# Spreading a position bias over query rows: single-partition transfers on ScalarE's queue, or scratch in HBM on GpSimd's

## The chip, the cores and the metric

One core of a Trainium2 chip runs the whole program: two layers of a first transformer block and two of a second, on 256 tokens of 1024 features. The metric is device time in microseconds (us), from the launch to the end of the program.

## What is computed

All of it is float32. In the part that the change touches, a feed-forward product is followed by an attention in windows, whose scores get a learned bias by relative position (cut from the reference):

```python
for i in range(DEPTH):                                    # DEPTH = 2
    h = x + 0.5 * swiglu(rms_norm(x, norm_ffn1[i]), w_ffn1_in[i], w_ffn1_out[i])
    u = rms_norm(h, norm_mix[i])
    q, k, v, c, g = jnp.split(u @ w_in[i], splits, axis=-1)
    ...
    y_attn = window_attention(q, k, v, sink[i], rel_bias) @ w_attn_out[i]
    ...

def window_attention(q, k, v, sink, rel_bias):            # BLOCK = WINDOW = 128, 8 heads
    ...
    rel = kj[None, :] - BLOCK - qi[:, None]               # qi: 128 query rows, kj: 384 key columns
    bias = rel_bias[t5_buckets(rel)]
    bias = bias.transpose(2, 0, 1).reshape(KV_HEADS, GROUP, BLOCK, 3 * BLOCK)
    s = s + bias[None, None]
    s = jnp.where(valid[None, :, None, None], s, NEG_INF)
    ...
```

The bias depends on `rel` alone. A head therefore needs one line of 511 numbers, of which query row r wants the 384 that begin at 127 - r. The same table serves both layers.

## The kernel before

**Tiling.** Tokens are columns, features are partitions: `h` is 128 x 8 x 256. Every product runs on 128 x 128 weight tiles against 256 columns. For precision each float32 weight is split into a high and a low part, and each tile takes three matmuls (`mm3`, lines 281 to 283).

**The weight stream.** `Stream` loads the weights in the order of a plan, in chunks of 128 x 2048 (1 MB) into three `raw` buffers, by transfers that SyncE's queue issues (line 198). Each chunk has two halves of 1024 columns. For each half ScalarE makes `wh` (line 221) and VectorE makes `wl` (line 222), in three buffers each. A half serves 24 matmuls in an output product. `wh` of a half waits until its `raw` has landed and until the matmuls of the half three before it are done.

**The stage in question.** `swiglu` runs an input product (line 405 writes its hidden values `hh`) and then an output product, `stage_o`, whose four results are added to `h` (line 442) on VectorE and squared for the next norm. The norm's mean goes to GpSimd, which raises it to the power -0.5 (`rt`, line 383). Then `mix1` runs its projections and the window attention, where VectorE reads the bias (line 511). The same stage stands in both layers, and the scheduler places the work of `bias_table()` at its start in layer 0.

**The bias table.** `bias_table()` is called once, after the first feed-forward part of layer 0. Two matmuls (line 1101) turn the one-hot matrix `oh` and the table `rl` into `tps`, 8 heads x 512 positions, and VectorE copies it to `tsb` (line 1103), one head to a partition. Then eight transfers of 192 KB each, issued by ScalarE's queue (line 1107), fill the two `bias` tiles of 128 x 4 x 384: each reads one partition of `tsb` 128 times, one element earlier for each query row, in runs of 384 numbers (1536 bytes).

**What sets the order.** Each engine runs its instructions in the order in which the scheduler wrote them, and an instruction that waits holds all that stand behind it on that engine. A transfer's issue is an instruction of the issuing engine's queue like any other.

Of the kernel before, what the change touches and what calls it, by code (L numbers as in the profile page):

```python
# [10 lines left out]
F32 = mybir.dt.float32  # L11
# [140 lines left out]
def build(ctx: ExitStack, tc: tile.TileContext, ws, xT, pT, vec, rbias, const, out):  # L152
    nc = tc.nc
# [7 lines left out]
    tmp = ctx.enter_context(tc.tile_pool(name="tmp", bufs=1))  # L161
    sm = ctx.enter_context(tc.tile_pool(name="sm", bufs=2))
    psm = ctx.enter_context(tc.tile_pool(name="psm", bufs=4, space=PSUM))
    side = {}

    def stile(shape, name):
        return side["s"].tile(shape, F32, tag="s", name=name)
# [4 lines left out]
    def f32(ap):  # L172
        return ap.bitcast(F32)

# [1 line left out]
    class Stream:  # L176
        RAW, LEAD = 3, 1

# [65 lines left out]

    W = Stream()

# [1 line left out]
    ident = cst.tile([128, 128], F32, name="ident")  # L248
    ones = cst.tile([128, 128], F32, name="ones")
    nv = VEC["_n"]  # L250
# [13 lines left out]
    def vc(name, l, i=0, n=1):  # L264
        a, _ = VEC[name, l]
        return vt[:, a + i:a + i + n]
# [1 line left out]
    mhalf = cst.tile([128, 32], F32, name="mhalf")  # L268
    S.activation(out=mhalf, in_=ones[:, 0:32], func=AF.Copy, scale=-0.5)

# [1 line left out]
    def cut(wh, wl, s):  # L272
        return wh[:, s], None if wl is None else wl[:, s]

# [47 lines left out]
                    mm3(o, (X.hi[k][:, s], X.lo[k][:, s]), (wh[:, a:b], wl[:, a:b]),  # L322
                        k == 0 and first, k == K - 1)

# [1 line left out]
    def new_h():  # L326
        return hp.tile([128, KD, T], F32, tag="h", name="h")

# [84 lines left out]
    def with_phase(name):  # L413
        def wrap(f):
            def go(*a):
                with phase(name) as P:
                    return f(P, *a)
            return go
        return wrap

# [1 line left out]
    @with_phase("ffn")  # L422
    def swiglu(P, l, which, h, norm, rb, nxt):
        hi, lo, A = hidden(P, 22)
# [46 lines left out]
        stage_o("w_down_2", l, 32, 26, A, evac_out)  # L471
        return h2

# [1 line left out]
    cur = {}  # L475

    def atile(name):
# [81 lines left out]
                    V.scalar_tensor_tensor(out=dl[:, j, :], in0=tp[:, j, :], scalar=gc, in1=f32(dh[:, j, :]),  # L559
                                           op0=ALU.mult, op1=ALU.subtract)  # L560

# [1 line left out]
    @with_phase("mix")  # L563
    def mix1(P, l, h, norm, nxt, ple):
        rt, rb = norm.finish()
# [139 lines left out]

        conv()

        # layer norm over channels, then silu
        def chan_sum(src, name):
            s2 = etile(name)  # L710
            V.tensor_tensor(out=s2, in0=src[:, 0:2, :], in1=src[:, 2:4, :], op=ALU.add)
            s1 = etile(name + "b")
            mark[name] = V.tensor_tensor(out=s1[:, 0:1, :], in0=s2[:, 0:1, :], in1=s2[:, 1:2, :], op=ALU.add)
            return s1

        R = tail.enter_context(phase("tail"))
        with tc.high_priority(offset=LN):
# [12 lines left out]
            for ct in range(4):  # L730
                S.activation(out=co[:, ct, :], in_=y[:, ct, :], func=AF.Silu, scale=vc("conv_ln_g", l, ct),
                             bias=vc("conv_ln_b", l, ct))
# [54 lines left out]
        stage_g("w_pe_gate", l, KD, G_PE, norm.act, evac)  # L787
        return h2

# [1 line left out]
    def rope_apply(dst, src, nh, dh, t, off):  # L791
        half = dh // 2
        cos = rope[:, t, off:off + half].unsqueeze(1).to_broadcast([128, nh, half])
        sin = rope[:, t, off + half:off + dh].unsqueeze(1).to_broadcast([128, nh, half])
        x1, x2 = src[:, :, 0:half], src[:, :, half:dh]
        ta = tmp.tile([128, nh, half], F32, tag="ra", name="ra", bufs=2)
        tb = tmp.tile([128, nh, half], F32, tag="rb2", name="rb2", bufs=2)
        tc_ = tmp.tile([128, nh, half], F32, tag="ra", name="ra", bufs=2)
        td = tmp.tile([128, nh, half], F32, tag="rb2", name="rb2", bufs=2)
        V.tensor_tensor(out=ta, in0=x1, in1=cos, op=ALU.mult)  # L800
        V.tensor_tensor(out=tb, in0=x2, in1=sin, op=ALU.mult)
        V.tensor_tensor(out=tc_, in0=x2, in1=cos, op=ALU.mult)
        V.tensor_tensor(out=td, in0=x1, in1=sin, op=ALU.mult)
        V.tensor_tensor(out=dst[:, :, 0:half], in0=ta, in1=tb, op=ALU.subtract)
        V.tensor_tensor(out=dst[:, :, half:dh], in0=tc_, in1=td, op=ALU.add)

    @with_phase("mixers")
    def mix2(P, l, h, norm, nxt):
# [67 lines left out]

            return [job(i) for i in range(3)]

        # mixer B, projections
        cq = P.tile([128, 2, 544], F32, name="cq")  # L880
        proj(G_B[0], [cq[:, t, 0:288] for t in range(2)])
        proj(G_B[1], [cq[:, t, 288:544] for t in range(2)])
# [11 lines left out]
        to_feature(cq[:, :, 0:512], 4, cT[:, 0], cT[:, 1], 0,  # L894
                   gain=lambda j: vc("mla_q_norm_g_2", l, j) if j < 3 else vc("mla_kv_norm_g_2", l))

        # mixer C, projections
        cc = P.tile([128, 2, 768], F32, name="cc")
        for i in range(3):
            proj(G_C[i], [cc[:, t, 256 * i:256 * i + 256] for t in range(2)])  # L900
# [4 lines left out]
        to_T(lambda t, j: cc[:, t, 128 * j:128 * j + 128], cqT[:, 0:2, :], 0, 2, 32 ** -0.5)  # L905
        to_T(lambda t, j: cc[:, t, 128 * j:128 * j + 128], cqT[:, 2:4, :], 2, 2, None)

        # mixer C, attention
        def combine(opc):
            oc = etile("oc")  # L910
            S.activation(out=oc.rearrange("p a b -> p (a b)"), in_=opc.rearrange("p t h d -> p (t h d)"), func=AF.Copy)
            sqc = etile("sqc")
            S.activation(out=sqc, in_=oc, func=AF.Square)
            ssc = sm.tile([128, 8], F32, tag="ssc", name="ssc")
            V.tensor_reduce(out=ssc, in_=sqc.rearrange("p a (h d) -> p (a h) d", d=64), op=ALU.add,
                            axis=mybir.AxisListType.X)
            msc = sm.tile([128, 8], F32, tag="msc", name="msc")
            V.tensor_scalar(out=msc, in0=ssc, scalar1=1.0 / 64, scalar2=1e-5, op0=ALU.mult, op1=ALU.add)
            rsc = sm.tile([128, 8], F32, tag="rsc", name="rsc")
            G.tensor_tensor(out=rsc, in0=msc, in1=mhalf[:, 0:8], op=ALU.pow)  # L920
            V.tensor_tensor(out=o_tok[:, :, 768:1024].rearrange("p a (h d) -> p a h d", d=64),
                            in0=oc.rearrange("p a (h d) -> p a h d", d=64),
                            in1=rsc.rearrange("p (a h) -> p a h", a=2).unsqueeze(3).to_broadcast([128, 2, 4, 64]),
                            op=ALU.mult)
            return lambda: to_feature(o_tok[:, :, 768:1024], 2, ho, lo, 6, gain=lambda j: subg[l])
# [64 lines left out]

        advance(STEPS[0])

        # mixer B, up-projections
        qb = P.tile([128, 2, 576], F32, name="qb")
        Xq = Act([cT[:, 0, k, :] for k in range(3)], [cT[:, 1, k, :] for k in range(3)])
        Xk = Act([cT[:, 0, 3, :]], [cT[:, 1, 3, :]])
# [22 lines left out]

        advance(STEPS[1])  # L1020

        # mixer A
        qa = P.tile([128, 2, 2, 384], F32, name="qa")
        va = P.tile([128, 2, 384], F32, name="va")
        for i in range(2):
# [26 lines left out]
        stage_o("w_o_2", l, KD, 5, Act([ho[:, k, :] for k in range(8)], [lo[:, k, :] for k in range(8)]), evac_o, CBA)  # L1052
        return h2

# [1 line left out]
    nA = Norm("norm_ffn1", 0)  # L1056
    for j in range(4):
        nA.prep(h, j)
# [32 lines left out]
    bias1 = [P1.tile([128, 4, 384], F32, name=f"bias{i}") for i in range(2)]  # L1091
    ple_out = P1.tile([128, 8, T], F32, name="ple")

    # relative position bias of every head, window columns -128..255 around each query block
    def bias_table():
        rl = cst.tile([33, 8], F32, name="rl")
        oh = tmp.tile([33, 512], F32, tag="e", name="oh", bufs=4)
        nc.sync.dma_start(out=rl, in_=rbias)
        nc.sync.dma_start(out=oh, in_=const["onehot"])
        tps = stile([8, 512], "tps")  # L1100
        PE.matmul(tps, rl, oh, start=True, stop=True)
        tsb = tmp.tile([8, 512], F32, tag="e", name="tsb", bufs=4)
        V.tensor_copy(out=tsb, in_=tps)
        for hd in range(8):
            base = tsb[hd:hd + 1, 127:511]
            src = bass.AP(tensor=base.tensor, offset=base.offset, ap=[list(base.ap[0]), [-1, 128], [1, 384]])
            nc.scalar.dma_start(out=bias1[hd // 4][:, hd % 4, :], in_=src)  # L1107

# [1 line left out]
    for l in range(DEPTH):  # L1110
        ple = {}
        _, rb = nA.finish()
# [38 lines left out]
        (nc.scalar if j % 2 else nc.sync).dma_start(out=out[:, 2 * j:2 * j + 2, :], in_=o)  # L1151


# [1 line left out]
def _consts():  # L1155
    ident = np.eye(128, dtype=np.float32)
    i = np.arange(T)
    dist = i[:, None] - i[None, :]
    causal = np.where(dist >= 0, 0.0, NEG2).astype(np.float32)
    mult = ((dist <= 128).astype(int) + (dist % 4 == 0) + (dist % 16 == 0)) * (dist >= 0)  # L1160
    logm = np.where(mult > 0, np.log(np.maximum(mult, 1)), NEG2).astype(np.float32)

    def rows(a):
        return a.reshape(2, 128, -1).transpose(1, 0, 2).reshape(128, -1)

    tabs = []
    for dim in (64, 32):
        half = dim // 2
        inv = (1.0 / (10000.0 ** (np.arange(half, dtype=np.float64) / half)))
        inv = inv.astype(np.float32)  # L1170
        ang = i.astype(np.float32)[:, None] * inv[None, :]
        tabs += [np.cos(ang.astype(np.float64)), np.sin(ang.astype(np.float64))]
    tabs = np.concatenate(tabs + [np.zeros((T, 96))], axis=1).astype(np.float32)
    blob = np.concatenate([ident, rows(causal), rows(logm), rows(tabs)], axis=1)

    rel = np.arange(512) - 255
    n = np.abs(rel)
    nf = np.maximum(n, 1).astype(np.float32)
    big = 8 + (np.log(nf / np.float32(8)) / np.float32(math.log(16)) * np.float32(8)).astype(np.int32)
    big = np.minimum(big, 15)  # L1180
    bucket = np.where(rel > 0, 16, 0) + np.where(n < 8, n, big)
    onehot = np.zeros((33, 512), np.float32)
    inside = n <= 128
    onehot[bucket[inside], np.arange(512)[inside]] = 1.0
    onehot[32, ~inside] = NEG1
    return np.ascontiguousarray(blob, dtype=np.float32), onehot
# [56 lines left out]
```

## Time and profile before

| what | value |
|---|---|
| median of three runs (1792.05 to 1794.16) | 1793.62 us |
| profiled execution, span from first to last instruction | 1792.7 us |
| TensorE busy | 1739.1 us, 97% |
| VectorE busy | 1182.9 us, 66% |
| ScalarE busy | 957.5 us, 53% |
| GpSimd busy | 27.9 us, 2% |
| mean granted TensorE clock | 0.989 of full speed |
| moved by the DMA engines | 302.91 MB, mean 169 GB/s |

The profiled execution is one more execution of the same program; of its own time the profile gives the span, which lies 0.9 us under the median. Busy time counts an engine's work, not the time in which its queue is held by an issue: ScalarE's held queue is named apart (ACTq). In rows of a timeline the columns are start, duration, engine, line, operation, tiles, and in brackets the idle time before with what ended it.

### The profile page before, as it was taken

What the parts mean: (1) busy time and instruction counts of PE and PEld (TensorE: products, weight loads), DVE (VectorE), ACT (ScalarE), POOL (GpSimd) and SP (SyncE); (2) the same over time, 40 slices, a digit from 0 to 9 for tenths busy, and PEclk for the clock granted to TensorE, in tenths of its full rate; (3) what the DMA queues carried; (4) which work ended last, traced back from release to release, by engine and by line L of the source; (5) the groups of instructions that cost most, each with busy time, mean ns of one, the idle gap of its engine ahead of it and who ended that gap; (6) DMA issues with size and microseconds to landing.
All of it is one profiled execution on the core that took longest, in us unless ns stands there. A gap on an engine that the chain in (4) does not pass through costs nothing.

```text
span 1792.7 us, 33450 instructions
## 1 busy us (share of the span) xinstructions
PE 1739.1 (97%) x14132; PEld 1705.3 (95%) x14132; DVE 1182.9 (66%) x1825; ACT 957.5 (53%) x1517; POOL 27.9 (2%) x25
## 2 busy tenths in 40 slices
PE   8996699999999999999999999999999999999998
PEld 8995699999999999999989999999899999999998
DVE  6662279867664866658877665678576557766644
ACT  5441258755444644456855444568555446755543
POOL 0000000000000000000000000000000000000000
PEclk9998799999999999999999999999999999999999
DMA  7557745254555544555334555544255554435552
GB/s 272 177 182 115 133 160 193 78 192 183 188 177 199 184 176 183 188 190 187 118 141 174 182 187 188 187 166 162 72 188 188 189 184 158 150 106 179 187 190 104
DMA packets 45598, 302.91 MB, mean 169 GB/s; under 512 B 5223, under 2 KB 6503, under 8 KB 12936
## 3 DMA queue, kind: packets, MB, share of 16 engines
q1 hardware_dynamic: 44008, 298.68, 47.1%
q10 hardware_dynamic: 1440, 2.10, 2.5%
q8 instruction: 110, 1.80, 0.4%
q14 instruction: 40, 0.33, 0.0%
HBM read 298.14 MB, written 1.05 MB: 167 GB/s over the span
## 4 chain that ended last, share of the span: by engine, by line
PE 91%; ACT 2%; ACTq 2%; DVE 2%; DMA 1%; issue 0%; POOLq 0%; DVEq 0%; SPq 0%
PE m L283 25%; PE m L282 25%; PE m L281 25%; ACTq L1107 2%; PE sp L508 2%; PE pa L283 2%; PE pa L282 2%; PE pa L281 2%; PE op L537 2%; PE m L279 1%; DVE wl L222 1%; PE tp L524 1%; ACT wh L221 1%; DMA raw<-in_ws_dram 1%; PE tpq L834 0%; PE qps L282 0%
## 5 line engine op out<-in xcount | busy, mean ns | idle before, releaser
L222 DVE TENSOR_TENSOR wl<-raw,wh 128x1024 fp32r<-128x1024 f32 (+3 forms) x565 | 674.9, 1198 | 507.4 <-ACT wh L221 505.9
L221 ACT ACTIVATE wh<-raw 128x1024 fp32r<-128x1024 f32 (+3 forms) x565 | 584.4, 1038 | 722.5 <-PE m L282 576.4
L281 PE MATMUL m<-xh,wh 128*128 128x256 f32 x2432 | 684.2, 284 | 7.4 <-ACT wh L221 7.4
L282 PE MATMUL m<-xl,wh 128*128 128x256 f32 x2432 | 687.6, 284 | 0.5 <-DVE xl L348 0.5
L283 PE MATMUL m<-xh,wl 128*128 128x256 f32 x2432 | 681.7, 284 | 0.0
L281 PEld LDWEIGHTS m<-xh,wh 128*128 128x128 f32 x2432 | 465.6, 192 | 8.0 <-ACT wh L221 7.4
L282 PEld LDWEIGHTS m<-xl,wh 128*128 128x128 f32 x2432 | 467.1, 192 | 1.5 <-DVE xl L348 0.9
L283 PEld LDWEIGHTS m<-xh,wl 128*128 128x128 f32 x2432 | 464.0, 192 | 1.3 <-issue 1.3
L281 PE MATMUL m<-hh,wh 128*128 128x256 f32 x1216 | 336.8, 279 | 31.3 <-ACT wh L221 31.3
L282 PE MATMUL m<-hl,wh 128*128 128x256 f32 x1216 | 336.3, 278 | 0.0
L283 PE MATMUL m<-hh,wl 128*128 128x256 f32 x1216 | 332.2, 279 | 1.9 <-DVE wl L222 1.7
L281 PEld LDWEIGHTS m<-hh,wh 128*128 128x128 f32 x1216 | 231.2, 190 | 32.8 <-ACT wh L221 32.8
L282 PEld LDWEIGHTS m<-hl,wh 128*128 128x128 f32 x1216 | 230.9, 190 | 0.0
L283 PEld LDWEIGHTS m<-hh,wl 128*128 128x128 f32 x1216 | 227.5, 190 | 3.3 <-DVE wl L222 3.3
L282 PE MATMUL pa<-wl,xh 128*128 128x256 f32 (+2 forms) x256 | 77.7, 307 | 0.5 <-DVE wl L222 0.5
L281 PE MATMUL pa<-wh,xh 128*128 128x256 f32 (+2 forms) x256 | 77.7, 310 | 0.0
L283 PE MATMUL pa<-wh,xl 128*128 128x256 f32 (+2 forms) x256 | 76.9, 308 | 0.0
L595 ACT ACTIVATE tap<-cpad,vt 128x256 f32<-128x256 f32 x120 | 53.6, 500 | 9.3 <-DVE acc L597 9.3
L606 DVE SCALAR_TENSOR_TENSOR acc<-cpad,vt,acc 128x256 f32<-128x256 f32 x120 | 52.7, 479 | 0.8
L282 PEld LDWEIGHTS pa<-wl,xh 128*128 128x128 f32 x256 | 48.3, 190 | 1.5 <-DVE wl L222 1.1
L281 PEld LDWEIGHTS pa<-wh,xh 128*128 128x128 f32 x256 | 48.1, 190 | 0.9 <-issue 0.7
L283 PEld LDWEIGHTS pa<-wh,xl 128*128 128x128 f32 x256 | 47.8, 190 | 0.4 <-issue 0.3
(255 smaller groups left out, 1882.9 us busy)
## 6 DMA issues: line engine op xcount, KB each, us to landing
raw<-in_ws_dram SPq DMA_DIRECT2D x254, 1024.0 KB, 4.8
raw<-in_ws_dram SPq DMA_DIRECT2D x18, 768.0 KB, 4.3
raw<-in_ws_dram SPq DMA_DIRECT2D x8, 896.0 KB, 4.6
raw<-in_ws_dram SPq DMA_DIRECT2D x2, 944.0 KB, 5.3
raw<-in_ws_dram SPq DMA_DIRECT2D x2, 864.0 KB, 4.6
raw<-in_ws_dram SPq DMA_DIRECT2D x2, 848.0 KB, 4.5
raw<-in_ws_dram SPq DMA_DIRECT2D x3, 512.0 KB, 7.2
bias<-tsb ACTq DMA_DIRECT2D x8, 192.0 KB, 24.4
```

The costliest lines, as they stand in the source:

```text
L221: S.activation(out=h[:, :b - a], in_=t[:, a:b], func=AF.Copy)
L222: V.tensor_tensor(out=lo[:, :b - a], in0=t[:, a:b], in1=f32(h[:, :b - a]), op=ALU.subtract)
L279: PE.matmul(o, wh, xh, start=first, stop=last, skip_group_check=True)
L281: PE.matmul(o, wh, xh, start=first, stop=False, skip_group_check=True)
L282: PE.matmul(o, wh, xl, start=False, stop=False, skip_group_check=True)
L283: PE.matmul(o, wl, xh, start=False, stop=last, skip_group_check=True)
L508: PE.matmul(sp[:, t, :n], q[:, 128 * t:128 * t + 128], k[:, :n], start=True, stop=True, skip_group_check=True)
L524: PE.transpose(tp[:, kt, 128 * t:128 * t + 128], pr[:, t, 128 * kt:128 * kt + 128], ident)
L537: PE.matmul(o[t], pt[:, kt, 128 * t:128 * t + 128], v[kt], start=(kt == 0), stop=(kt == nk - 1), skip_group_check=True)
L595: S.activation(out=pt[:, ct % 2, :], in_=cpad[:, ct, tap:tap + T], func=AF.Copy, scale=vc("conv_w", l, ct * TAPS + tap))
L606: V.scalar_tensor_tensor(out=y[:, ct, :], in0=src, scalar=wc, in1=y[:, ct, :], op0=ALU.mult, op1=ALU.add)
L1107: nc.scalar.dma_start(out=bias1[hd // 4][:, hd % 4, :], in_=src)
```

## The change

The eight transfers leave ScalarE's queue. In their place GpSimd issues ten: `tsb` goes to a line of 8 x 512 in HBM, that line is copied to `rep`, 8 x 128 x 512 in HBM (every head's line 128 times, 2 MB), and from `rep` eight loads fill the bias tiles. Each reads 128 rows of 384 numbers, at a step of 511 numbers, so that each row begins one position earlier in its own copy of the line.

```diff
+    drm = ctx.enter_context(tc.tile_pool(name="drm", bufs=1, space=bass.MemoryType.DRAM))
...
         tsb = tmp.tile([8, 512], F32, tag="e", name="tsb", bufs=4)
         V.tensor_copy(out=tsb, in_=tps)
+        line = drm.tile([8, 512], F32, name="line")
+        nc.gpsimd.dma_start(out=line, in_=tsb)
+        rep = drm.tile([8, 128, 512], F32, name="rep")
+        base = line[0:8, :]
+        src = bass.AP(tensor=base.tensor, offset=base.offset, ap=[[512, 8], [0, 128], [1, 512]])
+        nc.gpsimd.dma_start(out=rep, in_=src)
         for hd in range(8):
-            base = tsb[hd:hd + 1, 127:511]
-            src = bass.AP(tensor=base.tensor, offset=base.offset, ap=[list(base.ap[0]), [-1, 128], [1, 384]])
-            nc.scalar.dma_start(out=bias1[hd // 4][:, hd % 4, :], in_=src)
+            base = rep[hd]
+            src = bass.AP(tensor=base.tensor, offset=base.offset + 127, ap=[[511, 128], [1, 384]])
+            nc.gpsimd.dma_start(out=bias1[hd // 4][:, hd % 4, :], in_=src)
```

The rest of the diff takes out comments; below the added pool the lines of the program move down by one.

ScalarE's instructions in the program before, at the end of layer 0's first input product and the start of the output product (`wh` is the high half of the weights, `raw` the loaded weights):

```order
L405 ACTIVATE hh<-u 128x512
L221 ACTIVATE wh<-raw 128x1024 x3
L1107 DMA bias_150<-tsb 128x1x384
L221 ACTIVATE wh<-raw 128x1024
L1107 DMA bias_150<-tsb 128x1x384 x3
L1107 DMA bias_151<-tsb 128x1x384
L221 ACTIVATE wh<-raw 128x1024
L1107 DMA bias_151<-tsb 128x1x384 x3
L221 ACTIVATE wh<-raw 128x1024 x13
```

The same engine and place in the changed program:

```order
L431 ACTIVATE g<-g 128x512
L406 ACTIVATE hh<-u 128x512
L222 ACTIVATE wh<-raw 128x1024 x18
L347 ACTIVATE xh<-h,vt 128x256 x2
L356 ACTIVATE sq<-h 128x512
```

The 3 + 1 + 1 + 13 splits that stood around the eight issues now stand in one row of 18. On GpSimd, the changed program has from the first norm on:

```order
L384 TENSOR_TENSOR rt<-ms,mhalf 128x2
L1106 DMA line<-tsb 8x512
L1110 DMA rep<-line 1024x1x512
L1114 DMA bias_152<-rep 128x384 x4
L1114 DMA bias_153<-rep 128x384 x4
L384 TENSOR_TENSOR rt<-ms,mhalf 128x2
L637 TENSOR_TENSOR qrs<-qms,mhalf 128x20
```

The ten issues stand between the powers of the first and the second norm of layer 0, where GpSimd had nothing before. TensorE, VectorE and SyncE have the same instructions in the same order as before.

## Rows read from the trace of the kernel before

**Rows 1.** The page's 40 slices of the span: granted TensorE clock in tenths.

```profile
PEclk9998799999999999999999999999999999999999
```

**Rows 2.** The page's chain that ended last, shares by engine and line.

```profile
PE m L283 25%; PE m L282 25%; PE m L281 25%; ACTq L1107 2%; PE sp L508 2%; PE pa L283 2%; PE pa L282 2%; PE pa L281 2%; PE op L537 2%; PE m L279 1%; DVE wl L222 1%; PE tp L524 1%; ACT wh L221 1%; DMA raw<-in_ws_dram 1%; PE tpq L834 0%; PE qps L282 0%
```

**Rows 3.** ScalarE's timeline, layer 0's stage, and the last hh of layer 1.

```profile
140.50 0.63 ACT L405 ACTIVATE hh<-u 128x512 fp32r<-128x512 f32 x1 [2.10 <-DVE u L433]
...
147.77 0.60 ACTq L1107 DMA_DIRECT2D bias<-tsb  x1
...
148.97 20.14 ACTq L1107 DMA_DIRECT2D bias<-tsb  x4
169.23 1.06 ACT L221 ACTIVATE wh<-raw 128x1024 fp32r<-128x1024 f32 x1 [19.22 <-issue]
169.26 21.30 ACTq L1107 DMA_DIRECT2D bias<-tsb  x3
190.66 2.95 ACT L221 ACTIVATE wh<-raw 128x1024 fp32r<-128x1024 f32 x3 [20.37 <-DMA bias<-tsb]
...
746.27 0.63 ACT L405 ACTIVATE hh<-u 128x512 fp32r<-128x512 f32 x1 [2.10 <-DVE u L433]
```

**Rows 4.** Waits from 140 to 235 us: total, times, longest.

```profile
PE m L281 <- ACT wh L221: 31.3, 3, 15.6
...
ACT wh L221 <- DMA raw<-in_ws_dram: 9.2, 2, 8.6
...
PE m L283 <- DVE wl L222: 1.7, 3, 0.8
```

**Rows 5.** VectorE's timeline: tsb, and the stage's first h in each layer.

```profile
147.07 0.67 DVE L1103 COPY tsb<-tps 8x512 f32<-8x512 f32 x1
...
226.92 0.69 DVE L442 SCALAR_TENSOR_TENSOR h<-m,h 128x512 f32<-128x512 f32 x1
...
791.46 0.68 DVE L442 SCALAR_TENSOR_TENSOR h<-m,h 128x512 f32<-128x512 f32 x1
```

**Rows 6.** Windows: length, busy PE, PEld, DVE, ACT, POOL (instructions), PEclk, DMA share, GB/s.

```profile
140.50:226.92 86.42, 53.40 (x399) 51.04 (x398) 21.57 (x19) 18.09 (x18) 0.00 (x0) 0.80 0.76 121
746.27:791.46 45.19, 45.11 (x398) 44.91 (x397) 21.26 (x19) 18.47 (x18) 0.00 (x0) 1.00 0.55 195
```

**Rows 7.** The chain in order of time: start, duration, what.

```profile
145.08 0.95 PE tps L1101 x2
```

**Rows 8.** GpSimd's timeline: rt of the second norm in layers 0 and 1.

```profile
248.27 0.70 POOL L383 TENSOR_TENSOR rt<-ms,mhalf 128x2 f32<-128x2 f32 x1 [227.66 <-DVE ms L381]
...
812.33 0.69 POOL L383 TENSOR_TENSOR rt<-ms,mhalf 128x2 f32<-128x2 f32 x1 [180.39 <-DVE ms L381]
```

**Rows 9.** Instructions on the bias tiles: ns min/median/max, first and last start.

```profile
L511 DVE CUSTOM_DVE_ANT_0 pr<-sp,bias,nsink x32: 471/480/485, 307.1 to 892.5; 128x256 f32<-128x256 f32 x32
L1107 ACTq DMA_DIRECT2D bias<-tsb x8: 530/6226/8425, 147.8 to 183.2; - x8
```

**Rows 10.** DMA from 146 to 206 us: queue's packets, MB, share; KB each, us to landing.

```profile
q10 hardware_dynamic: 1143, 1.57, 71.1%
...
raw<-in_ws_dram SPq DMA_DIRECT2D x5, 1024.0 KB, 14.3
```

**Rows 11.** DMA from 0 to 60 us: KB each, us to landing.

```profile
rope<-in_blob_dram SPq DMA_DIRECT2D x1, 192.0 KB, 8.6
```

**Rows 12.** The page's DMA issues: KB each, median us to landing.

```profile
raw<-in_ws_dram SPq DMA_DIRECT2D x254, 1024.0 KB, 4.8
```

**Rows 13.** ScalarE's and VectorE's timelines in layer 1's stage.

```profile
764.74 1.06 ACT L221 ACTIVATE wh<-raw 128x1024 fp32r<-128x1024 f32 x1 [1.66 <-PE m L282]
...
765.84 1.22 DVE L222 TENSOR_TENSOR wl<-raw,wh 128x1024 fp32r<-128x1024 f32 x1 [1.49 <-ACT wh L221]
```

**Rows 14.** TensorE's timeline after the first stall, first and last matmul of a half.

```profile
170.34 0.58 PE L281 MATMUL m<-hh,wh 128*128 128x256 f32 x1 [13.21 <-ACT wh L221]
...
175.94 0.28 PE L283 MATMUL m<-hh,wl 128*128 128x256 f32 x1
```

## Prediction

> **What bounds the kernel now.** Read the page's 40 slices first: the granted TensorE clock is full everywhere except in two neighbouring slices, at about 134 to 224 us, where it falls to 7 and 8 tenths [rows 1]. Then the chain that ended last: it is TensorE's matmuls nearly everywhere, and the only entry near the top that is neither a matmul nor weight handling is ScalarE's own queue at line 1107, with 2% of the span [rows 2]. Line 1107 issues the eight bias transfers. So the place to look at is one stage, the first feed-forward output product of layer 0.
>
> ScalarE's timeline there shows what happens [rows 3]. The first bias transfer is issued in 0.60 us at 147.77. The next four hold ScalarE's queue for 20.14 us, and the three after them for 21.30 us, until 190.66. Between them stand weight splits (wh, line 221), which run one at 169.23 and the next at 190.66; without wh neither the rest (wl, VectorE) nor the matmuls can go on. TensorE waits 31.3 us in three waits for wh and 1.7 us for wl [rows 4].
>
> How much of that is the transfers' doing can be read from layer 1, which runs the same stage on the same shapes with no bias table. I take as marks the last hidden split of the input product (hh, line 405) and the first residual addition (h, line 442): 140.50 to 226.92 in layer 0, 746.27 to 791.46 in layer 1 [rows 3, 5]. These are 86.42 and 45.19 us; TensorE is busy 53.40 of the one and 45.11 of the other, at mean clocks of 0.80 and 1.00 [rows 6]. So layer 0 is **41.23 us** longer: 33.0 us in which TensorE stands idle, and 8.3 us in which its matmuls take longer, after each stall at the lower clock.
>
> **The change part by part.** *Taken away:* eight DMA issues on ScalarE and the wait for wh behind them. Of the 41.23 us, 0.95 us belong to the two table matmuls at line 1101, which the chain counts at that price [rows 7]; they stay. What goes is 41.23 - 0.95 = **40.3 us**, if the stage then runs as in layer 1. In the built order the instructions of TensorE and VectorE are the same ones in the same order, ScalarE's are the same less the eight issues, and SyncE's loads are the same; so layer 1 is a fair model of what is left.
>
> *Added on GpSimd:* ten issues (line, rep, eight bias), of which rep waits for line to land and the first bias for rep. Ahead of them GpSimd has nothing to do (its idle time before rt is 227.66 us), and next after them stands rt (line 383), at 248.27 before [rows 8] and so about 208 after. No row shows an issue by GpSimd. The nearest are ScalarE's first at 0.60 us and its worst at 8.43 us, a blocked one [rows 3, 9]: ten make 6 to 84 us. I take 1 us each, 10 us, near the first, because what held ScalarE's queue was a backlog of slow transfers that the new source does not have.
>
> *Added on the DMA engines:* rep writes 2 MB from HBM to HBM, bias loads 8 x 192 KB from HBM. The old transfers had 1536-byte runs from one partition: 1143 packets took 71.1% of 16 engines for 60 us [rows 10], that is 0.711 x 16 x 60 / 1143 = 0.60 us each. A load of the same size and run length from HBM, rope, 192 KB, landed in 8.6 us in the crowd of the program's first loads [rows 11]; a weight load of 1 MB lands in 4.8 us [rows 12]. Cheap end for rep: two weight loads, 9.6 us. Dear end: 1024 packets of 0.60 us on 16 engines, 38 us, and doubled if it shares them with the weights, 76 us. The bias loads: 8 of 8.6 us one after another, 69 us, at the dear end, and 1.5 x 4.8 = 7 us at the cheap end. I take 20 us for rep and 20 us for the eight, because source and target are contiguous HBM rows as in the weight loads. Then: tsb ready at 147.8 [rows 5], line landed at about 151 (an estimate: one issue and a landing like that of a small load), rep at 171, last bias issue at 180, last landing near 195. The cover is 13 us or more before rt at 208, and, as the bias is first read by line 511 at 307.1 before [rows 9], so at 266.8 after, about 70 us before that.
>
> [...]
>
> *The weights beside it.* The weight queue has to keep 1 MB per 5.44 us. In layer 1 a wh starts every 2.72 us (1.06 us of work after 1.66 us of waiting for TensorE); its wl is done 2.3 us after the start (764.74 to 765.84 + 1.22) [rows 13] and frees the raw buffer; the same buffer's next wh comes five halves later, 13.6 us. That leaves 11.3 us for a landing that takes 4.8, so 6.5 us of slack, and TensorE takes a half two halves after its buffer came free, 5.4 - 2.3 = 3.1 us more. A weight load may therefore double to 9.6 us and cost nothing; if the cover is gone, it costs rival A. I take nothing for it.
>
> *Sum.* The profiled execution's span is 1792.7; 1792.7 - 40.3 = 1752.4. The median of the runs shown is 0.9 us above that span, so the forecast for the median is **1753.3 us**. The layers stay alike behind the stage: from the first h to the next rt it is 21.35 us in layer 0 and 20.87 in layer 1 [rows 5, 8], so what this comparison leaves open is about 0.5 us, and I leave it out of the sum.
>
> **The rivals.** *A: the weights come late beside rep and bias.* For it: in the bias stretch of before, weight loads landed in a median of 14.3 us, against 4.8 [rows 10, 12], and ScalarE waited 9.2 us for raw [rows 4]. Against it: those shared the engines with 0.60 us packets from one partition. At 14.3 us, three buffers turn over in 14.3 + 5.0 = 19.3 us in place of 16.3, 1 us lost per chunk of 5.44 us; over 76 us that is 14 chunks, 14 us: up to **1767**, and I think of it as 1757 to 1767. Chance 0.11.
>
> *B: GpSimd's descriptor work and VectorE get in each other's way.* VectorE's wl has the 3.1 us of slack above. If the issue of rep, the largest, held it as long as ScalarE's worst issue, 8.4 us, that costs 5.3 us and a restart at the lower clock. At such a restart the 24 matmuls of a half ran from 170.34 to about 176.1 [rows 14], some 5.7 us in place of 2.72: 3 us more, **1761 to 1762**. Against it: no row shows VectorE held by GpSimd. Chance 0.05. [...]
>
> *C, the slower side: the two-step spread through HBM ends too late.* If HBM to HBM shares the engines as badly as the old transfers did with the weights (14.3 / 4.8 = 3 times), rep takes 38 x 3 = 115 us and lands at 266; the bias loads land 38 to 115 us later, at 304 to 381, where line 511 wants them at 266.8, and rt has stood behind rep on GpSimd's queue since 208. The loss is 38 to 115 us, the time 1791 to 1868, about **1830**. It decides from where the last bias lands after 266.8 + 40.3 = 307. Chance 0.05, of which 0.04 slower and 0.01 within no change. That the change does not do what it says is no case by itself: the issues are off ScalarE's queue in the built order.
>
> **How the numbers follow.** Forecast as summed, 1751 to 1757: 0.79; A 0.11, B 0.05, C 0.05. What a measurement of this kernel can tell from no change is about 0.2%, 3.6 us. Faster by more: 0.79 + 0.11 + 0.05 = 0.95; same 0.01; slower 0.04. The range: below, the whole 41.23 us gone and the lower of the runs (1792.05 - 41.2 = 1750.8), so 1750.5; above, 1761, which takes in the forecast's own bounds and the cheap part of A.
>
> **What would show it.** ScalarE's timeline after 147 should have a wh every 2.72 us with no gap; the stage from hh at about 140.5 to h should be 46 us, at full clock; GpSimd's queue should end its issues by about 190, with rt at 208; weight loads in the stage should land in under 11 us; line 512 (511 before) should not wait for bias. A weight load over 11 us would speak for A, a wl that waits on nothing visible for B, rt after 210 or a wait for bias for C. The prediction is wrong if the stage is longer than about 50 us, or if the time goes elsewhere.

## The result and the profile after

| | median | runs | profiled span |
|---|---|---|---|
| before | 1793.14 us | 1792.05 to 1794.16 | 1792.7 us |
| changed | 1754.34 us | 1753.97 to 1754.68 | 1752.3 us |

The ratio is 0.978 (95% interval 0.9766 to 0.9794): 38.8 us less in the medians, 40.4 us less in the two profiled spans.

The page of the changed kernel, its clock slices, the transfers that GpSimd issued (queue, packets, MB, share of 16 engines) and the chain:

```profile
PEclk9999999999999999999999999999999999999999
...
q0 software_dynamic: 1584, 3.69, 0.6%
...
PE m L284 26%; PE m L283 26%; PE m L282 26%; PE sp L509 2%; PE pa L284 2%; PE pa L283 2%; PE pa L282 2%; PE op L538 2%; PE m L280 1%; PE tp L525 1%; DVE wl L223 1%; ACT wh L222 1%; PE tpq L835 0%; PE qps L283 0%; PE qps L282 0%; PE qps L284 0%
```

The two low slices of [rows 1] are gone, and so is ScalarE's queue from the head of the chain [rows 2]. The stage between the same two marks, from hh at 140.51 to the first h, as VectorE's timeline and the window (columns as in [rows 6]) have it:

```profile
186.50 0.68 DVE L443 SCALAR_TENSOR_TENSOR h<-m,h 128x512 f32<-128x512 f32 x1
```

```profile
140.50:186.50 46.00, 46.00 (x400) 45.02 (x399) 21.84 (x19) 18.47 (x18) 6.13 (x10) 1.00 0.76 274
```

It was 86.42 us at a mean clock of 0.80 and is 46.00 us at full clock, TensorE busy throughout: layer 1's 45.19 us and the table's matmuls. ScalarE's timeline now has a wh every 2.72 us (two of the row of 18):

```profile
151.62 1.06 ACT L222 ACTIVATE wh<-raw 128x1024 fp32r<-128x1024 f32 x1 [1.66 <-PE m L283]
...
173.38 1.06 ACT L222 ACTIVATE wh<-raw 128x1024 fp32r<-128x1024 f32 x1 [1.66 <-PE m L283]
```

GpSimd's timeline, with its ten issues:

```profile
148.05 0.71 POOL L1106 DMA_DIRECT2D line<-tsb  x1 [126.96 <-DVE tsb L1104]
152.41 1.11 POOL L1110 DMA_DIRECT2D rep<-line  x1 [3.65 <-DMA line<-tsb]
173.95 4.30 POOL L1114 DMA_DIRECT2D bias<-rep  x8 [20.42 <-DMA rep<-line]
207.30 0.71 POOL L384 TENSOR_TENSOR rt<-ms,mhalf 128x2 f32<-128x2 f32 x1 [29.05 <-DVE ms L382]
```

The bracket before rt is the cover, the time by which GpSimd could be later at no cost: GpSimd waited 29.05 us for the norm, not the norm for GpSimd. The transfers from 146 to 200 us (KB each, median us to landing):

```profile
raw<-in_ws_dram SPq DMA_DIRECT2D x10, 1024.0 KB, 4.9
rep<-line POOLq DMA_DIRECT2D x1, 2048.0 KB, 21.2
bias<-rep POOLq DMA_DIRECT2D x8, 192.0 KB, 4.5
line<-tsb POOLq DMA_DIRECT2D x1, 16.0 KB, 4.1
```

The landings of weight loads (min, median, max), first all of the program and then the three issued from 156 to 168 us, while `rep` was being copied:

```profile
DMA to landing us min/median/max: 4.1/4.8/9.3
```

```profile
DMA to landing us min/median/max: 7.0/8.0/9.1
```

The bias transfers on the page of before:

```profile
bias<-tsb ACTq DMA_DIRECT2D x8, 192.0 KB, 24.4
```

A bias load that took 24.4 us from one partition takes 4.5 us from HBM. The median weight load of this stretch lands in 4.9 us (14.3 in [rows 10]); beside the copy to `rep` it takes 7.0 to 9.1.

### The profile page after: what moved, and what is told of

Its sections match the earlier page's. It is cut to its first block, busy times and chain, and to the rows that moved or that the text cites. A ratio compares the mean times of both kernels' runs of the same rounds, so it can differ in the third digit from the quotient of the medians.

```text
span 1752.3 us, 33467 instructions
## 1 busy us (share of the span) xinstructions
PE 1731.5 (99%) x14132; PEld 1698.7 (97%) x14132; DVE 1183.1 (68%) x1825; ACT 958.2 (55%) x1517; POOL 34.1 (2%) x35
## 3 DMA queue, kind: packets, MB, share of 16 engines
q0 software_dynamic: 1584, 3.69, 0.6%
## 4 chain that ended last, share of the span: by engine, by line
PE 95%; ACT 2%; DVE 2%; DMA 0%; issue 0%; SPq 0%; POOLq 0%; DVEq 0%; ACTq 0%
PE m L284 26%; PE m L283 26%; PE m L282 26%; PE sp L509 2%; PE pa L284 2%; PE pa L283 2%; PE pa L282 2%; PE op L538 2%; PE m L280 1%; PE tp L525 1%; DVE wl L223 1%; ACT wh L222 1%; PE tpq L835 0%; PE qps L283 0%; PE qps L282 0%; PE qps L284 0%
## 6 DMA issues: line engine op xcount, KB each, us to landing
rep<-line POOLq DMA_DIRECT2D x1, 2048.0 KB, 21.2
```

## The experiments

The change does two things at once: another source (HBM rows in place of one partition of `tsb`) and another issuing engine. The prediction priced the hold of ScalarE's queue and named the slow packets as its cause, but it never asked what each half brings alone.

**Only the engine changes.**

```diff
-            nc.scalar.dma_start(out=bias1[hd // 4][:, hd % 4, :], in_=src)
+            nc.gpsimd.dma_start(out=bias1[hd // 4][:, hd % 4, :], in_=src)
```

> The kernel before with one edit: the eight single-partition transfers are issued by GpSimd instead of ScalarE's queue; nothing goes through HBM. It changes the queue alone. Theory Q (the held ScalarE queue is what cost 40 us, the slow transfers themselves are second): ScalarE's wh keep their 2.72 us pace for as long as weights land, the stage takes 46 to 57 us (weights late beside the old transfers by up to 1 us per chunk of 5.44 us, some 11 chunks), time 1754 to 1766. Theory S (the slow source is what cost it, by holding up the DMA engines, and ScalarE's hold only hides that): weight loads land in 14 us or more, ScalarE waits for raw instead of for its queue, time 1780 to 1793.

Measured: 1795.6 us beside 1793.88 of before, ratio 1.0012 (1.0003 to 1.0022). Nothing is gained. GpSimd's and ScalarE's timelines:

```profile
148.31 4.42 POOL L1107 DMA_DIRECT2D bias<-tsb  x8 [127.74 <-DVE tsb L1103]
```

```profile
160.03 1.06 ACT L221 ACTIVATE wh<-raw 128x1024 fp32r<-128x1024 f32 x1 [1.66 <-PE m L282]
206.95 2.01 ACT L221 ACTIVATE wh<-raw 128x1024 fp32r<-128x1024 f32 x2 [45.86 <-DMA raw<-in_ws_dram]
```

All eight issues are done in 4.42 us, ScalarE is free, and it waits 45.86 us for weights instead. TensorE's wait (total, times, longest), the weight loads, and the bias transfers' landings (min, median, max):

```profile
PE m L281 <- ACT wh L221: 39.8, 1, 39.8
```

```profile
raw<-in_ws_dram SPq DMA_DIRECT2D x5, 1024.0 KB, 46.2
```

```profile
DMA to landing us min/median/max: 10.8/33.9/55.2
```

Ten microseconds in the middle of the wait (columns as in [rows 6]):

```profile
180.00:190.00 10.00, 0.00 (x0) 0.00 (x0) 0.00 (x0) 0.00 (x0) 0.00 (x0) 0.50 0.95 34
```

A weight load lands in 46 us in place of 4.8, and the 16 DMA engines are busy for 95% of the time while they move 34 GB/s (76% at 274 GB/s in the changed kernel's stage). Theory S holds and theory Q falls, although the time lies 2.6 us above the 1780 to 1793 of theory S: in the kernel before, ScalarE's held queue was one face of the same backlog, and had ScalarE not waited for its queue it would have waited for weights.

**Only the source changes.** The changed kernel, with `nc.scalar` for `nc.gpsimd` in its three `dma_start` lines (line, rep and the eight loads).

> The changed kernel with one edit: line, rep and the eight bias loads are issued by ScalarE's queue instead of GpSimd. It changes the source alone, but the wait for rep now stands on ScalarE's queue. In the built order the first bias load stands behind eight wh of the stage, so ScalarE gets to it at about 161, and rep lands at about 174. Theory Q (any wait on ScalarE's queue costs, whatever its cause): ScalarE is held 13 us, the next wh is 12.7 us late, TensorE has 4.4 us of cover, so it stalls 8 us and restarts at the lower clock for 2 to 3 us more: 1764 to 1766. Theory S (the slow source is what cost): the queue is free, about 1754.

Measured: 1764.49 us. The source alone brings 1793.88 - 1764.49 = 29.4 us, and the other 10.2 us to the changed kernel are the wait for rep on the wrong queue. ScalarE's timeline, TensorE's wait, and the window after it (columns as in [rows 6]):

```profile
160.01 1.06 ACT L222 ACTIVATE wh<-raw 128x1024 fp32r<-128x1024 f32 x1 [1.66 <-PE m L283]
172.69 0.82 ACTq L1114 DMA_DIRECT2D bias<-rep  x2
173.63 1.06 ACT L222 ACTIVATE wh<-raw 128x1024 fp32r<-128x1024 f32 x1 [12.56 <-DMA rep<-line]
```

```profile
PE m L282 <- ACT wh L222: 6.5, 1, 6.5
```

```profile
174.00:178.00 4.00, 2.79 (x11) 2.50 (x12) 2.11 (x2) 2.66 (x3) 0.00 (x0) 0.50 0.87 288
```

The time came out as computed for theory Q: a wait of 12.6 us on ScalarE (13 expected), 6.5 us of TensorE (8 expected), and a restart at the lower clock (0.50 in this window). So both theories hold a part: the source decides whether there is a backlog, and the engine decides who stands behind the one wait that the new way has.

**ScalarE issues, without that wait.** Line and rep on GpSimd, the eight loads on ScalarE, held back by two small copies in the convolution.

```diff
+        if "go" in late:
+            for i in range(2):
+                V.tensor_copy(out=bias1[i][:, :, 0:1], in_=cpad[:, :, PAD:PAD + 1])
+            late.pop("go")()
...
-            nc.gpsimd.dma_start(out=bias1[hd // 4][:, hd % 4, :], in_=src)
+            nc.scalar.dma_start(out=bias1[hd // 4][:, hd % 4, :], in_=src)
...
+            late["go"] = lambda: bias_loads(rep)
```

> The changed kernel with line and rep issued by GpSimd as there, and the eight bias loads issued by ScalarE's queue again, but in the convolution's part, where rep has long landed (two small VectorE copies into the bias tiles hold them back until then). The source is HBM and ScalarE issues, without a wait. If ScalarE's queue as such is no cost and only what it waits for is: eight issues of about 0.45 us, none on TensorE's path, 1754 to 1756. If eight issues on ScalarE's queue cost by themselves: 1758 or more.

Measured: 1754.0 us (1753.48 to 1754.28), the changed kernel's time. ScalarE's queue there:

```profile
226.31 0.83 ACTq L1122 DMA_DIRECT2D bias<-rep  x2
...
228.08 2.33 ACTq L1122 DMA_DIRECT2D bias<-rep  x5
...
230.53 0.58 ACTq L1122 DMA_DIRECT2D bias<-rep  x1
```

Eight issues on ScalarE, 3.7 us in all, cost nothing that the time shows when nothing is waited for.

**How much cover there is.** The copy to rep three times in a row, in the changed kernel.

```diff
-        nc.gpsimd.dma_start(out=rep, in_=src)
+        for _ in range(3):
+            nc.gpsimd.dma_start(out=rep, in_=src)
```

> The changed kernel with the copy to rep done three times in a row, each after the one before has landed. It tells how much cover GpSimd's chain has. By the changed kernel's trace one copy takes 21.2 us to land, rep is complete at about 217 instead of 174, the bias issues end at about 222, and rt, which stands behind them at 207.3, ends at 222.5. TensorE's transposes of rt stood at 210.3 and would be 12 us late, with a restart at the lower clock: 1766 to 1769 if TensorE has no other work to put in between, as its fixed order says. The rival, that the 29 us between the bias issues and rt are not the whole cover, since the bias itself is not read before 266: no cost, 1754.

Measured: 1766.48 us. GpSimd's and TensorE's timelines:

```profile
215.97 4.34 POOL L1115 DMA_DIRECT2D bias<-rep  x8 [17.01 <-DMA rep<-line]
220.30 0.77 POOL L384 TENSOR_TENSOR rt<-ms,mhalf 128x2 f32<-128x2 f32 x1
```

```profile
221.12 0.69 PE L392 MATMUL pb<-ident,rt 128*128 128x128 f32 x2 [10.37 <-POOL rt L384]
```

rt comes 13 us later than in the changed kernel, TensorE stands 10.37 us, and the time grows by 12.1 us. The cover is the 29 us ahead of rt and some 2 us behind it. Beyond that, 10.4 us of stall and a slower restart (from 221.8 to 223.5 us the matmuls are recorded with 0.41 us each, from 223.9 us with 0.28) cost 12.1 us in this run, while the bias itself was not yet late.

**The floor.** No transfers at all; the bias tiles are zeroed by GpSimd, so that the scores lack bias and mask.

> The changed kernel without the ten transfers; the bias tiles are set to zero by GpSimd instead, so the scores lack their bias and mask. It is the floor: what is left to gain if the spread cost nothing at all. If the spread is wholly hidden behind the weight stream: the same time as the changed kernel, 1754 within 1 us. If the DMA traffic of rep and bias still costs (rival A of the prediction): below it by what that costs, 1745 to 1752. It also tells whether the time around the span, 1.8 us in the changed kernel, has to do with transfers by GpSimd.

Measured: 1753.93 us (1752.91 to 1754.57). The medians differ by 0.4 us, less than the runs of one kernel do: the 3.7 MB of the spread cost nothing that these runs can tell, and rival A did not come.

**Bytes or runs?** The first experiment's kernel, 192 of the 384 columns of each transfer, the other half of the bias left at zero.

```diff
+        for t in bias1:
+            G.memset(t, 0.0)
...
-            src = bass.AP(tensor=base.tensor, offset=base.offset, ap=[list(base.ap[0]), [-1, 128], [1, 384]])
...
+            src = bass.AP(tensor=base.tensor, offset=base.offset, ap=[list(base.ap[0]), [-1, 128], [1, 192]])
+            nc.gpsimd.dma_start(out=bias1[hd // 4][:, hd % 4, 0:192], in_=src)
```

> As the run with the single-partition transfers on GpSimd, but every transfer takes 192 of the 384 columns (the other half of the bias is left at zero): the same number of runs, half the bytes of each. In the full run the eight transfers occupied the engines for about 58 us and TensorE stalled 39.8 us. Theory P (what limits is the bytes that one partition can give, about 27 GB/s): the transfers take about 29 us, the stall falls by about 29 to some 11 us, time 1765 to 1770. Theory N (what limits is the number of runs, a fixed price each): no change, 1793 to 1797.

Measured: 1769.94 us; bias landings, and TensorE's stall:

```profile
DMA to landing us min/median/max: 7.0/17.6/25.9
```

```profile
178.83 0.58 PE L281 MATMUL m<-hh,wh 128*128 128x256 f32 x1 [10.14 <-ACT wh L221]
```

Half the bytes in as many runs take half the time, so theory N falls. Taking the longest landing in both kernels as that of the last issue, the full set moved 1.57 MB from 148.3 to 152.2 + 55.2 = 207.4, 26.6 GB/s, and this one 0.79 MB in 29.8 us, 26.4 GB/s. The limit is bytes per second, and it lies with the source, since the same bytes from HBM into the same tiles landed in 4.5 us.

**Which partitions?** Three runs with GpSimd issuing from single partitions. First on partitions 0, 4, 8 to 28 (zero columns between the heads in `rl`):

```diff
-        rl = cst.tile([33, 8], F32, name="rl")
+        rl = cst.tile([33, 32], F32, name="rl")
+        G.memset(rl, 0.0)
...
-        nc.sync.dma_start(out=rl, in_=rbias)
+        nc.sync.dma_start(out=rl[:, 0:32:4], in_=rbias)
...
-            base = tsb[hd:hd + 1, 127:511]
+            base = tsb[4 * hd:4 * hd + 1, 127:511]
...
```

> As the run with the single-partition transfers on GpSimd, but the eight heads' lines lie on partitions 0, 4, 8 to 28 instead of 0 to 7; each transfer still reads one partition. Theory P1 (the engines work the transfers off in order, so at any moment all of them read one partition, and where it lies doesn't matter): the same 27 GB/s, the same stall of about 40 us, 1793 to 1797. [...]

Then on partitions 0 to 3 and 32 to 35 (zero columns between them again):

```diff
...
-            base = tsb[hd:hd + 1, 127:511]
+            q = hd % 4 + 32 * (hd // 4)
+            base = tsb[q:q + 1, 127:511]
...
```

> As the run with the heads' lines on partitions 0, 4, 8 to 28 and GpSimd issuing, but on partitions 0 to 3 and 32 to 35. The first run with partitions 0 to 7 had its last transfer land after 55.2 us, the one with 0, 4 to 28 after 21.0 us. [...] Theory D (what matters is how far apart the partitions lie, in other words two clusters of four as in 0 to 7): the same as partitions 0 to 7, 55 us and 1793 to 1797, or less.

Then 0 to 7 again in another order:

```diff
-        for hd in range(8):
+        for hd in (0, 4, 1, 5, 2, 6, 3, 7):
...
```

> As the run with partitions 0 to 7 and GpSimd issuing, with one edit: the heads are issued in the order 0, 4, 1, 5, 2, 6, 3, 7. The same partitions, the same bytes. With partitions 0 to 7 in order the last transfer landed after 55.2 us, with 0 to 3 and 32 to 35 after 57.8 us, with 0, 4 to 28 after 21.0 us. Theory G2 (partitions 0 to 3 share one path and 4 to 7 another; in the old order neighbours in the queue read the same path, so one path worked at a time): neighbours now read two paths, the last lands after about 28 us, TensorE stalls some 10 us, time 1765 to 1772. Theory D (the eight lie too close together, whatever the order): again about 55 us, 1793 to 1798.

Measured: 1763.3, 1801.11 and 1774.98 us. The bias landings (min, median, max) of the three, one fence each in this order:

```profile
DMA to landing us min/median/max: 9.2/15.8/21.0
```

```profile
DMA to landing us min/median/max: 9.9/35.2/57.8
```

```profile
DMA to landing us min/median/max: 10.4/24.7/32.8
```

And TensorE's stall in the first and the third:

```profile
172.67 0.58 PE L281 MATMUL m<-hh,wh 128*128 128x256 f32 x1 [5.19 <-ACT wh L221]
```

```profile
184.29 0.58 PE L281 MATMUL m<-hh,wh 128*128 128x256 f32 x1 [16.34 <-ACT wh L221]
```

In the first, theory P1 fell: spreading the lines more than doubles the rate (1.57 MB in 24.9 us, 63 GB/s in place of 26.6), so it does matter where they lie. In the second, theory D was near: the last landing came after 57.8 us against 55.2, but the time of 1801.11 us lies 4 us above the 1793 to 1797. The third decides. The order alone, with the same partitions and bytes, takes the last landing from 55.2 to 32.8 us and 20.6 us off the time. Theory D had no change for that edit, so it falls. In the old order most neighbours in the queue read from the same four partitions; the second run kept that order and only moved the second four from 4 to 7 to 32 to 35, which changed little (55.2 and 57.8 us). The landing at 32.8 us, the stall of 16.34 and the time of 1774.98 were all above the forecasts of theory G2 (28, some 10, and 1765 to 1772). The runs show what order and place do to the landings; the two paths of theory G2 were a supposition, and no run shows them.

**The same on ScalarE's queue:** the kernel before with only that edit to 0, 4 to 28.

> The kernel before with the heads' lines on partitions 0, 4, 8 to 28 instead of 0 to 7, and ScalarE's queue still issuing: only the place of the source changes. In the kernel before the eight issues held ScalarE for 41.4 us between them. If that hold is the backlog of slow transfers, it shrinks as the transfers do (55.2 to 21.0 us with GpSimd), to 16 to 20 us in two pieces of 8 to 10, each with 4.4 us of cover: TensorE stalls 8 to 12 us and restarts twice for 3 us each, time 1765 to 1773. If ScalarE's queue holds because eight issues of such a pattern cost it that much themselves: no change, 1790 to 1794. If a queue takes the transfers strictly one after another, so that only one partition is read at a time: little change too, 1785 to 1794.

Measured: 1775.45 us (1773.15 to 1778.19), a little over the forecast 1765 to 1773. ScalarE's timeline from the second issue on:

```profile
148.92 15.13 ACTq L1108 DMA_DIRECT2D bias<-tsb  x4
164.17 1.06 ACT L221 ACTIVATE wh<-raw 128x1024 fp32r<-128x1024 f32 x1 [14.21 <-DMA raw<-in_ws_dram]
164.19 10.17 ACTq L1108 DMA_DIRECT2D bias<-tsb  x3
174.47 2.95 ACT L221 ACTIVATE wh<-raw 128x1024 fp32r<-128x1024 f32 x3 [9.24 <-DMA bias<-tsb]
```

The seven issues after the first, which held ScalarE for 41.4 us in [rows 3], hold it for 25.3, and the transfers land in a median of 12.8 us in place of 24.4: the hold follows the backlog, though it did not fall to the 16 to 20 us that I had expected. The first of the two gaps now ends with the weights.

**Another layout for rep.** The changed kernel with `rep` as 128 x 8 x 512.

```diff
-        rep = drm.tile([8, 128, 512], F32, name="rep")
+        rep = drm.tile([128, 8, 512], F32, name="rep")
...
-        src = bass.AP(tensor=base.tensor, offset=base.offset, ap=[[512, 8], [0, 128], [1, 512]])
+        src = bass.AP(tensor=base.tensor, offset=base.offset, ap=[[0, 128], [512, 8], [1, 512]])
...
-            base = rep[hd]
-            src = bass.AP(tensor=base.tensor, offset=base.offset + 127, ap=[[511, 128], [1, 384]])
+            base = rep[0, hd:hd + 1, :]
+            src = bass.AP(tensor=base.tensor, offset=base.offset + 127, ap=[[4095, 128], [1, 384]])
```

> The changed kernel with rep laid out as 128 x 8 x 512, so that the copy's outermost dimension is 128 instead of 8; the same bytes. In the changed kernel rep took 21.2 us to land. If the outermost dimension of 8 keeps it on 8 of the 16 engines, rep lands in 11 to 15 us here; if not, again in about 21 us. The time stays at 1754 in either case, since rep ends long before anything waits for it.

Measured: 1753.9 us, no change in time, and the copy lands in half of it. GpSimd's timeline and the transfer:

```profile
163.30 4.27 POOL L1114 DMA_DIRECT2D bias<-rep  x8 [10.32 <-DMA rep<-line]
```

```profile
rep<-line POOLq DMA_DIRECT2D x1, 2048.0 KB, 10.6
```

The layout halves the landing, 21.2 to 10.6 us, near the 11 to 15 us expected if the outermost 8 had kept the copy on 8 engines. On how many engines either copy ran no run shows, and the layout also changed the packets: GpSimd's queue moved its 3.69 MB in 688 of them, in place of 1584. The shorter landing leaves 11 us more of GpSimd's cover, but this kernel's time does not show it.

## Why the prediction was right, and where it was not

- **The sum** (1792.7 - 40.3 = 1752.4 for the span): measured 1752.3. Reading the stage against its twin in layer 1 was worth more than adding up stalls, because it holds the idle time, the slow clock after it (0.80 on average over the stage) and whatever replaced the wait. That the spans agree to 0.1 us is in part luck: between the medians it is 38.8 us.
- **The step from span to median** was mis-sized by 1.0 us. I added the 0.9 us between the profiled span of before and the median. Runs that have a time and a span of the same execution differ by 1.8 us (the changed kernel's profiled run: 1754.07 and 1752.3; the run without transfers: 1754.57 and 1752.8). So the profiled execution of before was a longer one than the median of the runs shown, by some 0.9 us, and the forecast for the median, 1753.3, came out that much under 1754.34.
- **"Taken away: eight DMA issues on ScalarE and the wait for wh behind them"**: the size was right and the cause half right. Moving the issues alone brought nothing (1795.6). What had to go was the source; the queue matters only for the wait on rep (10 us, 1764.5 against 1754.3).
- **GpSimd's chain**: rep in 20 us (21.2), ten issues of 1 us (0.71, 1.11 and 4.30 for eight), last issue at 180 (178.3). No row gave the landing of line, estimated for about 151; it took 4.1 us, to 152.2. Landings of the eight were taken too dear: 4.5 us each and overlapped, so that the last came 9 us after the first issue, in place of 20 us for all. rt stood at 207.3, as computed. The 20 us for rep were right by luck: the reason was contiguous rows, and the same copy on another layout took 10.6.
- **Rival A** did not come, but the copy to rep used most of its room: weight loads beside it landed in up to 9.1 us, inside the 11.3 us that the prediction left for a landing. But its price was far too low for the transfers it was taken from. I used the 14.3 us of [rows 10]; with ScalarE free those transfers held weight loads for 46 us. In the kernel before ScalarE's stall had kept the next loads from being asked for, so its landings showed the backlog too small. SyncE's issues from 152 to 206 us (ns min, median, max, first and last start), in the kernel before and in the one that changes only the engine:

```profile
L198 SPq DMA_DIRECT2D raw<-in_ws_dram x3: 328/2494/5104, 193.0 to 202.2; - x3
```

```profile
L198 SPq DMA_DIRECT2D raw<-in_ws_dram x2: 8752/10701/12650, 156.9 to 165.8; - x2
```

  In the kernel before, no load was asked for from 152 us until 193.0. With ScalarE free two were, at 156.9 and 165.8, and the backlog held even their issues for 8.75 and 12.65 us.
- **Rival B** did not come: the stage has TensorE busy for all of its 46.00 us, and the kernel without transfers has the same time.
- **Rival C** named the right place, but set its point too late. It said that the last bias must land by 307. The run with three copies puts the point where GpSimd is done with its issues, at about 210 (rt at 207.3 and the 2 us behind it), since rt stands behind them.

## What to carry to other kernels

When a queue is held at an issue, ask what the transfers behind it wait for before moving the issue: here a slow source also starved the weight queue (a load landed in 46 us in place of 4.8), and with ScalarE freed the wait came back under another name (45.86 us for weights). Price a whole stage against an undisturbed twin of it in the same trace, and then test the halves of a change one at a time. A dependent transfer belongs on a queue where whatever stands behind its wait comes late: the wait for rep cost 10 us on ScalarE's queue, and nothing that the time shows on GpSimd's.

## What the runs showed of the hardware that I had not expected

- Eight transfers that each read one partition, issued in order from partitions 0 to 7, moved 26 to 27 GB/s together, whichever queue issued them: 26.6 on GpSimd's, and on ScalarE's 1.57 MB from 147.8 to 183.2 + 25.0 = 208.2 us, 26.0. A 1 MB weight load on SyncE's queue beside them landed in 46 us in place of 4.8.
- The order of issue counts: such transfers land after 55.2 us in order and after 32.8 us when neighbours in the queue come from different groups of four.
- Issues on ScalarE's queue were cheap for the first two such transfers only: 0.60 us [rows 3] and 0.53 [rows 9], then 4.50 for the third and 8.43 for the fourth (the chain of before, below). From the fourth on the five took 36.5 us, 7.3 us each, and 192 KB at 26.6 GB/s take 7.4: about the pace at which the transfers end.

```profile
149.53 4.50 ACTq L1107
154.06 8.43 ACTq L1107
```
